# The first transfers and the first scaling step of a two-layer encoder kernel, and the place of ScalarE's squares in its MLP heads

## The chip, the cores and the metric

The kernel runs on one core of a Trainium2 chip. The metric is the device time of one execution in microseconds (us); three timed executions of the kernel before the change gave 1661.46 to 1661.52 us, median 1661.48 us. TensorE (PE) does the matrix products into PSUM, VectorE (DVE) and ScalarE (ACT) evacuate PSUM and prepare operands, GpSimd (POOL) does small side work, SyncE (SP) issues most DMAs; ACT and POOL issue some DMAs too. All times of the trace below are from the span's start.

## What is computed

Two independent sequences of 512 tokens with 1024 features go through two layers with the same weights. Layer 0 mixes by a grouped 2-D Fourier transform, layer 1 by grouped-query attention; each is followed by a squared-ReLU MLP of width 4096, and a final normalisation follows.

```
def sq_relu_mlp(h, w_up, w_down):
    a = jnp.maximum(h @ w_up, 0)
    return (a * a) @ w_down

for i in range(DEPTH):
    if i % N_MIXERS == 0:
        x = x + fourier_mix(rms_norm(x, fourier_norm[j]), fourier_w_out[j])
    else:
        x = x + gqa_attention(rms_norm(x, attn_norm[j]), ...)
    x = x + sq_relu_mlp(rms_norm(x, mlp_norm[i]), mlp_w_up[i], mlp_w_down[i])
return rms_norm(x, final_norm)
```

All data are float32. Most products are made from operands split into a rounded high half and a low rest, as three products of type float32r (high by high, high by low, low by high).

## The kernel before, in words

**The start.** `begin` issues the first loads. SP loads `g` (the gain of the first norm, 128x8 numbers, 4 KB), then the second token tile of `x`, the table `exact[0]` of cosines and sines (128x772), two more token tiles, and the tables `exact[1]` and `exact[2]`; ACT's queue loads the first token tile of `x` (512 KB, into `w`). While these come in, PE runs products of a constant tile with no use for the result (`idle`, line 622; first 12 of them, later 20). Between these two groups PE transposes the broadcast columns of `g` (line 392, 8 products), which puts the gain along the free dimension in PSUM. Then, for the first token tile: ACT squares and sums the row (line 445), POOL raises the mean to the power -0.5 (line 450), DVE multiplies the tile by the gain from PSUM (line 459, two halves), adds the two halves of the features (`plus`, line 463) and subtracts them (`minus`, line 472), and ACT scales the results by the row's factor (`scale_both`, line 484: for the first tile the first 128 columns of the sum, its other 384, 40 picked columns, the difference). The first real products (`exact_even`, line 547) use the scaled sum as weights, 128 columns for each of four output blocks, and the first 258 columns of `exact[0]` as the moving operand. Every instruction of the start is placed by hand, engine by engine.

**The MLP head.** The up product is done by Strassen-like block sums over the two sequences. `first_product` handles 16 pairs of blocks of `w_up`; the first eight form the head. For each pair p of the head, `first` makes the product of the pair's first weight block with `b11` (12 matmuls into one PSUM bank, line 1046) and ACT copies the bank to SBUF (line 1081, `blocks.copied`); `second` then goes on accumulating 12 more matmuls with `b21` into the same bank, so its first matmul must wait until ACT's copy has read the bank. ACT then applies Relu from PSUM (line 1062) and squares the result in place in SBUF (line 1063, `squared`); the square is followed by the DMA that spills it to DRAM for the later down product (line 1059, on ACT's queue). On PE `pair.second` of pair p-1 or p stands between other products, so that PE has matmuls of the next pair to do while ACT copies. For p below 3 the order on PE is that of the code; from there on a scheduler orders every engine's instructions by its own cost model, and `behind(x, y)` only tells it that x is to be placed after y. Before the change, in layer 1 alone and from p = 4 on, pair p-1's square was placed behind pair p's copy.

**The group of two in layer 1's down product.** `second_product` walks over groups of four blocks, one of two in layer 1. `puts` holds the low-half subtractions (line 87, DVE) of operands that were fetched for the next group; for the group of two, the second of the four was placed behind the first row's addition of a PSUM bank into its accumulator (`rows[0].added`, line 1269).

Of the kernel before, what the change touches and what calls it, by code (L numbers as in the profile page):

```python
# [16 lines left out]
ALU = mybir.AluOpType  # L17
# [27 lines left out]
def trunk_kernel(ctx, tc, x_in, xt_in, y_out, tables, rope, gfour, gcol, grow, gfin,  # L45
# [28 lines left out]
    def ps():  # L74
        return psp.tile([P, 512], F32, tag="ps", name=nm("ps"))
# [287 lines left out]

    def exact_table(k):
        t = slot([P, D], F32)
        nc.sync.dma_start(t[:, : tables[k].shape[-1]], tables[k])
        exact.append(t)

    def w_pair(src, n, a):
# [5 lines left out]
    def begin():  # L375
        gr, g = slot([P, D], F32), cons.tile([P, KC], F32, name="g")
        nc.sync.dma_start(g, gfour)
        load_x(0, 0, nc.scalar)
        load_x(0, 1)
        exact_table(4)  # L380
        for t in range(2, 4):
            load_x(0, t)
        exact_table(5)
        exact_table(6)
        nc.scalar.preload_act_table_set("natural_log_exp_and_others")
        idle(ps(), 12)
        halves = []
        for i in range(2):
            o = ps()
            for k in range(4):  # L390
                c = 4 * i + k
                nc.tensor.transpose(o[:, k * P : (k + 1) * P], g[:, c : c + 1].broadcast_to([P, P]), ident)
            halves.append(o)
        return gr, halves
# [36 lines left out]
    class Front:  # L431
# [46 lines left out]
        def scale_both(self, i):  # L478
            if i == 0:
                self.n = exact[0][:, 772:852].rearrange("p (i a b) -> p i a b", i=2, a=5)  # L480
            p, m = self.p[i], self.m[i]
            first = ((p[:, :P], p[:, :P]), (p[:, P:], p[:, P:])) if i == 0 else ((p, p),)
            for out, x in first + ((self.n[:, i], eights(m)), (m, m)):
                nc.scalar.activation(out, x, AF.Copy, scale=self.r[:, i : i + 1])
                yield
            parts.append((self.p[i], self.m[i], self.n[:, i]))
# [310 lines left out]
    with tc.manual_schedule(engines={ET.PE, ET.Activation, ET.DVE, ET.Pool, ET.SP}):  # L797
# [6 lines left out]
        wn.load()  # L804
        idle(ps(), 20)
        for i in range(2):
# [246 lines left out]
    def first_product(l, blocks, rows, ahead, head=iter(())):  # L1053
# [122 lines left out]
        for p in range(AHEAD):  # L1176
# [13 lines left out]
            with tc.manual_schedule(engines={ET.PE}) if p < 3 else nullcontext():  # L1190
                pair.first()
                if l and p > 3:
                    behind(pairs[p - 1].squared, blocks.copied)
# [56 lines left out]
    def second_product(l, blocks, rows, late=lambda: None, ready=lambda m: None, head=iter(())):  # L1250
# [214 lines left out]
        for k, (rows, sums) in enumerate(items):  # L1465
# [46 lines left out]
            if rows and rows[0].n == 2 and len(puts) == 4:  # L1512
                behind(puts[1], rows[0].added)
            for r in rows:
# [730 lines left out]
```

## Time and profile before

| what | value |
|---|---|
| median of three timed executions | 1661.48 us |
| the profiled execution's own time | 1660.31 us |
| its span from first to last instruction | 1658.5 us |
| mean granted TensorE clock | 0.999 |
| busy time PE / weight loads / DVE / ACT / POOL | 1651.5 / 1378.5 / 1265.0 / 878.3 / 394.1 us |
| DMA over the span | 301.43 MB, mean 182 GB/s |

The profiled execution took 1.81 us more than its span and 1.17 us less than the median of the timed ones. A row of the timeline gives the start, the duration, the engine, the line and operation, the tiles it writes and reads without their numbers, its size, the count of instructions merged into it, and in square brackets how long the engine was idle before it and what ended that. "PEld" is the weight load that goes ahead of each matmul; an engine name with a q (SPq) is that engine issuing a DMA. Matmuls are pipelined, so that PE's busy time hides short stalls: a wait shows in the idle time of PEld, and in a stretch that holds fewer matmuls than its length allows.

### The profile page before, as it was taken

The numbers are of one execution on the slowest core, as the hardware profiler recorded it, in microseconds if no ns is written. First come the engines' busy times: TensorE is split into PE (matmuls) and PEld (weight loads), VectorE is DVE, ScalarE is ACT, GpSimd is POOL, SyncE is SP. The second block draws the span as 40 slices with busy tenths as digits, with TensorE's granted clock in tenths as the row PEclk, the third lists the DMA queues.
The fourth block names the chain that finished last, engine by engine and source line by source line (L and its number), as shares of the span: only waits on it lengthen the run. The fifth ranks groups of instructions, "written<-read, shape, count | busy, mean of one in ns | idle before, by whom it ended". The sixth has DMA issues, their size and how long they took to land.

```text
span 1658.5 us, 22101 instructions
## 1 busy us (share of the span) xinstructions
PE 1651.5 (100%) x7762; PEld 1378.5 (83%) x7762; DVE 1265.0 (76%) x1797; ACT 878.3 (53%) x1551; POOL 394.1 (24%) x377
## 2 busy tenths in 40 slices
PE   9999999999999999999999999999999999999998
PEld 8988888888888888888888888888888888888887
DVE  8898785557886779868788888877855487878875
ACT  7776454446243425447688856554554552433335
POOL 5311443222000001325454303004422220000002
PEclk9999999999999999999999999999999999999999
DMA  9843554459775757425501146335544696756632
GB/s 313 241 172 108 196 210 165 146 193 371 229 237 172 246 180 228 177 66 199 166 1 39 65 175 231 127 108 180 201 149 168 226 366 200 233 163 221 186 114 103
DMA packets 121904, 301.43 MB, mean 182 GB/s; under 512 B 12312, under 2 KB 13720, under 8 KB 121792
## 3 DMA queue, kind: packets, MB, share of 16 engines
q1 hardware_dynamic: 98864, 253.66, 43.8%
q0 software_dynamic: 8528, 20.01, 5.7%
q10 hardware_dynamic: 14400, 26.35, 4.2%
q8 instruction: 61, 1.00, 0.2%
q14 instruction: 51, 0.42, 0.1%
HBM read 217.07 MB, written 82.38 MB: 181 GB/s over the span
## 4 chain that ended last, share of the span: by engine, by line
PE 98%; DVE 1%; issue 0%; ACT 0%; DMA 0%; POOL 0%; POOLq 0%; DVEq 0%; ACTq 0%
PE ps L1046 76%; PE ps L83 6%; PE ps L81 6%; PE ps L82 6%; PE ps L1657 2%; PE ps L1636 0%; PE ps L550 0%; PE ps L547 0%; DVE u L2002 0%; DMA g<-gfour 0%; PE ps L217 0%; PE ps L622 0%; PE ps L760 0%; PE ps L1626 0%; PE ps L587 0%
## 5 line engine op out<-in xcount | busy, mean ns | idle before, releaser
L1046 PE MATMUL ps<-u,w 128*128 128x512 f32 x4920 | 1124.6, 389 | 0.0
L1046 PEld LDWEIGHTS ps<-u,w 128*128 128x128 f32 x4920 | 922.7, 188 | 193.8 <-ACT u L1081 1.9
L86 ACT CAST w<-raw 128x1024 fp32r<-128x1024 f32 (+1 forms) x215 | 212.4, 993 | 309.6 <-PE ps L1046 235.9
L87 DVE TENSOR_TENSOR w<-raw,w 128x1024 fp32r<-128x1024 f32 (+1 forms) x215 | 249.3, 1164 | 66.6 <-ACT w L86 62.6
L86 ACT CAST u<-u 128x1024 fp32r<-128x1024 f32 (+1 forms) x140 | 140.7, 1046 | 84.9 <-PE ps L1046 37.4
L87 DVE TENSOR_TENSOR u<-u,u 128x1024 fp32r<-128x1024 f32 (+1 forms) x140 | 168.9, 1233 | 21.6 <-ACT u L86 20.7
L1046 PE MATMUL ps<-u,u 128*128 128x512 f32 x624 | 148.6, 389 | 0.0
L1296 POOL DMA_DIRECT2D raw<-w_sum x32 | 28.1, 879 | 468.5 <-DMA raw<-w_sum 167.6
L1166 POOL TENSOR_TENSOR u<-u 128x512 f32<-128x512 f32 x28 | 37.8, 1351 | 427.6 <-ACT u L1063 427.6
L1269 DVE TENSOR_TENSOR u<-ps,u 128x512 f32<-128x512 f32 x160 | 109.4, 685 | 36.8 <-PE ps L1046 34.0
L1046 PEld LDWEIGHTS ps<-u,u 128*128 128x128 f32 x624 | 117.1, 188 | 24.3
L81 PE MATMUL ps<-u,u 128*128 128x512 f32 (+2 forms) x342 | 129.0, 379 | 0.0
L83 PE MATMUL ps<-u,u 128*128 128x512 f32 (+2 forms) x342 | 124.5, 364 | 0.0
L82 PE MATMUL ps<-u,u 128*128 128x512 f32 (+2 forms) x342 | 124.2, 363 | 0.0
L177 POOL TENSOR_TENSOR t<-t,t 128x512 f32<-128x512 f32 (+1 forms) x47 | 67.5, 1441 | 187.2 <-ACT t L171 163.2
L1062 ACT ACTIVATE t<-t 128x512 f32<-128x512 f32 x64 | 40.5, 632 | 111.4 <-DVE t L1135 101.4
L87 DVE TENSOR_TENSOR u<-ps,u 128x512 fp32r<-128x512 f32 (+3 forms) x112 | 68.1, 635 | 7.3 <-ACT u L86 6.9
L83 PEld LDWEIGHTS ps<-u,u 128*128 128x128 f32 x342 | 64.3, 188 | 10.5 <-DVE u L87 0.4
L82 PEld LDWEIGHTS ps<-u,u 128*128 128x128 f32 x342 | 64.6, 189 | 8.5 <-DVE u L87 0.7
L81 PEld LDWEIGHTS ps<-u,u 128*128 128x128 f32 x342 | 64.7, 189 | 7.8
L1122 DVE TENSOR_TENSOR t<-ps,u 128x512 f32<-128x512 f32 x32 | 22.0, 687 | 60.9 <-PE ps L1046 50.3
L86 ACT CAST u<-ps 128x512 fp32r<-128x512 f32 (+3 forms) x112 | 59.4, 558 | 9.6 <-PE ps L1657 7.6
(270 smaller groups left out, 2013.3 us busy)
## 6 DMA issues: line engine op xcount, KB each, us to landing
raw<-w_up SPq DMA_DIRECT2D x80, 512.0 KB, 4.6
u<-spill_t SPq DMA_DIRECT2D x60, 512.0 KB, 7.0
raw<-w_sum SPq DMA_DIRECT2D x56, 512.0 KB, 5.6
u<-spill_b SPq DMA_DIRECT2D x45, 512.0 KB, 6.4
spill_t<-u SPq DMA_DIRECT2D x84, 256.0 KB, 2.0
spill_b<-t ACTq DMA_DIRECT2D x60, 256.0 KB, 4.2
raw<-w_row SPq DMA_DIRECT2D x28, 512.0 KB, 4.8
park<-u SPq DMA_DIRECT2D x24, 512.0 KB, 3.9
```

What stands on the lines that cost most here:

```text
L81: nc.tensor.matmul(out, lh, rh, start=first, stop=False)
L82: nc.tensor.matmul(out, lh, rl, start=False, stop=False)
L83: nc.tensor.matmul(out, ll, rh, start=False, stop=last)
L86: hi = nc.scalar.copy(dst_hi, src)
L87: return hi, eng.tensor_sub(dst_lo, src, f32(dst_hi))
L177: nc.gpsimd.tensor_add(acc[q][:, :n], acc[q][:, :n], s[:, :n])
L1046: nc.tensor.matmul(o, w[x][:, sl], h[k][y], start=first and k + i == 0, stop=k == n - 1 and i == 2, skip_group_check=not first)
L1062: nc.scalar.activation(t, src, AF.Relu)
L1166: eng.tensor_sub(t[:, 0], b12, b11)
L1269: return nc.vector.tensor_add(x, o, x)
L1296: nc.gpsimd.dma_start(s[:, 1], w[:, 3], accum_op=ALU.add)
L1657: nc.tensor.transpose(pt[:, t * P : (t + 1) * P], probs[t][:, sc * P : (sc + 1) * P], ident)
```

## The change

Three places are edited.

1. **The start.** `g` is loaded by ACT's queue and the first token tile by SP's, first of all. `exact_table` can load a table in pieces; the first 258 columns of `exact[0]` are now loaded ahead of the second token tile and the other 514 behind it. The idle products are 10 and 21 instead of 12 and 20. Of the first tile's four scaling steps, the first (128 columns of the sum) goes to DVE, where it stands behind `minus` of the same tile; the other steps stay on ACT.
2. **The MLP heads.** In both layers, from p = 3 on, pair p-1's square stands behind pair p's copy.
3. **The group of two.** All four of `puts`, not only the second, stand behind `rows[0].added`.

```diff
-    def exact_table(k):
+    def exact_table(k, cuts=()):
         t = slot([P, D], F32)
-        nc.sync.dma_start(t[:, : tables[k].shape[-1]], tables[k])
         exact.append(t)
+        edges = [0, *cuts, tables[k].shape[-1]]
+        for c0, c1 in zip(edges, edges[1:]):
+            nc.sync.dma_start(t[:, c0:c1], tables[k][:, c0:c1])
+            yield
...
     def begin():
-        nc.sync.dma_start(g, gfour)
-        load_x(0, 0, nc.scalar)
+        nc.scalar.dma_start(g, gfour)
+        load_x(0, 0)
+        pieces = exact_table(4, (258,))
+        next(pieces)
         load_x(0, 1)
-        exact_table(4)
+        for _ in pieces:
+            pass
...
-        idle(ps(), 12)
+        idle(ps(), 10)
...
-            for out, x in first + ((self.n[:, i], eights(m)), (m, m)):
-                nc.scalar.activation(out, x, AF.Copy, scale=self.r[:, i : i + 1])
+            for j, (out, x) in enumerate(first + ((self.n[:, i], eights(m)), (m, m))):
+                if i == j == 0:
+                    nc.vector.tensor_scalar(out, x, self.r[:, :1], None, ALU.mult)
+                else:
+                    nc.scalar.activation(out, x, AF.Copy, scale=self.r[:, i : i + 1])
                 yield
...
-        idle(ps(), 20)
+        idle(ps(), 21)
...
                 pair.first()
-                if l and p > 3:
+                if p > 2:
                     behind(pairs[p - 1].squared, blocks.copied)
...
             if rows and rows[0].n == 2 and len(puts) == 4:
-                behind(puts[1], rows[0].added)
+                for y in puts:
+                    behind(y, rows[0].added)
```

On SP's queue at the start of the program these are the first rows before (`u_109` is the second token tile, `u_111` the table `exact[0]`, `u_113` and `u_115` the third and fourth tile, `u_117` the table `exact[1]`):

```order
L377 DMA g<-gfour 128x8
L352 DMA u_109<-x 128x1024
L366 DMA u_111<-xtab 128x772
L352 DMA u_113<-x 128x1024
L352 DMA u_115<-x 128x1024
L366 DMA u_117<-xtab 128x770
```

And these now (`w_106` is the first token tile, `u_109` now the table, `u_111` the second token tile):

```order
L352 DMA w_106<-x 128x1024
L369 DMA u_109<-xtab 128x258
L352 DMA u_111<-x 128x1024
L369 DMA u_109<-xtab 128x514
L352 DMA u_114<-x 128x1024
L352 DMA u_116<-x 128x1024
```

The first token tile has come from ACT's queue to the head of SP's, a third of the table stands ahead of the second token tile, and `g` has gone to ACT's queue.

On ACT in layer 0's head, around pairs 3 and 4 (`u_1417`, `u_1457` and `u_1491` are the results of pairs 2, 3 and 4, `ps_` their banks; L1062 and L1063 are Relu and square, L1081 the copy), before:

```order
L1062 ACTIVATE u_1417<-ps_1418 128x512
L1059 DMA spill_b_0_1274<-u_1357 128x512
L1063 ACTIVATE u_1417<-u_1417 128x512
L1081 COPY u_1457<-ps_1458 128x512
L1059 DMA spill_b_0_1274<-u_1417 128x512
L86 CAST w_1584<-raw_1582 128x1024
L1062 ACTIVATE u_1457<-ps_1458 128x512
L86 CAST w_1630<-raw_1578 128x1024
L1063 ACTIVATE u_1457<-u_1457 128x512
L1081 COPY u_1491<-ps_1492 128x512
```

And now (L1072, L1073 and L1091 are the same three lines):

```order
L1072 ACTIVATE u_1417<-ps_1418 128x512
L1069 DMA spill_b_0_1274<-u_1357 128x512
L1091 COPY u_1457<-ps_1458 128x512
L1073 ACTIVATE u_1417<-u_1417 128x512
L1069 DMA spill_b_0_1274<-u_1417 128x512
L86 CAST w_1584<-raw_1582 128x1024
L1072 ACTIVATE u_1457<-ps_1458 128x512
L86 CAST w_1630<-raw_1578 128x1024
L1091 COPY u_1491<-ps_1492 128x512
L1073 ACTIVATE u_1457<-u_1457 128x512
```

Each square has changed places with the copy behind it.

On PE in the same head, between the last matmuls of pair 4's first product (weights from `u_1072` and `w_1488`, bank `ps_1492`) and the first of its second (`u_1092`), there stood six matmuls of pair 5 (`ps_1536`):

```order
L1046 MATMUL ps_1492<-u_1073,w_1488 128x512
L1046 MATMUL ps_1492<-u_1072,w_1488 128x512
L1046 MATMUL ps_1536<-u_1052,w_1532 128x512
L1046 MATMUL ps_1536<-u_1053,w_1532 128x512
L1046 MATMUL ps_1536<-u_1052,w_1532 128x512 x2
L1046 MATMUL ps_1536<-u_1053,w_1532 128x512
L1046 MATMUL ps_1536<-u_1052,w_1532 128x512
L1046 MATMUL ps_1492<-u_1092,w_1488 128x512
```

Now there stand four:

```order
L1056 MATMUL ps_1492<-u_1073,w_1488 128x512
L1056 MATMUL ps_1492<-u_1072,w_1488 128x512
L1056 MATMUL ps_1536<-u_1052,w_1532 128x512
L1056 MATMUL ps_1536<-u_1053,w_1532 128x512
L1056 MATMUL ps_1536<-u_1052,w_1532 128x512 x2
L1056 MATMUL ps_1492<-u_1092,w_1488 128x512
```

The scheduler has moved the second product two matmuls closer to the copy it waits for. The same count falls from six to four for pair 3 and from 14 to seven for pair 5 of layer 0; in layer 1 it falls from five to four for pair 3, stays at four for pair 4 and falls from six to five for pair 5.

More of the change, by code (lines that the diff above doesn't have):

```diff
@@ L376, in begin @@
         gr, g = slot([P, D], F32), cons.tile([P, KC], F32, name="g")
-        nc.sync.dma_start(g, gfour)
-        load_x(0, 0, nc.scalar)
+        nc.scalar.dma_start(g, gfour)
+        load_x(0, 0)
+        pieces = exact_table(4, (258,))
+        next(pieces)
         load_x(0, 1)
-        exact_table(4)
+        for _ in pieces:
+            pass
         for t in range(2, 4):
             load_x(0, t)
-        exact_table(5)
-        exact_table(6)
+        for k in (5, 6):
+            for _ in exact_table(k):
+                pass
         nc.scalar.preload_act_table_set("natural_log_exp_and_others")
-        idle(ps(), 12)
+        idle(ps(), 10)
         halves = []
```

## The prediction

> **What bounds the kernel now.** I read the page first, then who waits for whom among PE's weight loads, then the chain that ended last for the two heads, and last the timeline of the three places that the change touches. The page:
>
> ```profile
> span 1658.5 us, 22101 instructions
> ...
> PE 1651.5 (100%) x7762; PEld 1378.5 (83%) x7762; DVE 1265.0 (76%) x1797; ACT 878.3 (53%) x1551; POOL 394.1 (24%) x377
> ...
> PE 98%; DVE 1%; issue 0%; ACT 0%; DMA 0%; POOL 0%; POOLq 0%; DVEq 0%; ACTq 0%
> ```
>
> PE is busy all through, and the chain that ended last is 98% PE. The change leaves the number of useful matmuls as it is, so it can only move the moment at which PE's useful work starts, and the stalls inside PE's stream. The waits of the weight loads, in all the span, show how little there is of these:
>
> ```profile
> PEld ps L1046 <- ACT u L1081: 1.9, 7, 0.4
> PEld ps L622 <- DVE w L347: 1.2, 1, 1.2
> PEld ps L82 <- DVE u L87: 0.7, 4, 0.2
> ...
> PEld ps L547 <- ACT t L484: 0.2, 1, 0.2
> ```
>
> The first row is the wait that the squares' new place is about: seven times, 1.9 us in all, a second product of an MLP head waits for ACT's copy of the bank. Of the start there are 1.2 us ahead of the first idle product and 0.2 us ahead of the second block of the first real product (line 547); the 0.7 us for line 87 lie outside the touched places. No wait of the down products of layer 1 (DVE, line 87 or 1269) is in the list. So the whole field for a gain is about 2 us, or 0.1%. A measurement of this kernel can tell about 0.2% (3.3 us) from no change; the forecast is no change.
>
> **The start.** The timeline:
>
> ```profile
> 0.72 0.41 ACTq L352 DMA_DIRECT2D w<-x  x1
> 0.73 0.39 SPq L377 DMA_DIRECT2D g<-gfour  x1
> ...
> 1.16 2.93 PE L622 MATMUL ps<-u 128*128 128x256 f32 x12 [1.16 <-DVE w L347]
> ...
> 4.32 1.23 PE L392 MATMUL ps<-ident,g 128*128 128x128 f32 x8 [0.23 <-DMA g<-gfour]
> 4.89 1.06 ACT L445 ACTIVATE w<-w 128x1025 bf16<-128x1025 f32 x1 [2.44 <-DMA w<-x]
> 5.16 1.28 DVE L459 TENSOR_TENSOR u<-w,ps 128x512 f32<-128x512 f32 x2 [3.99 <-PE ps L392]
> ...
> 5.31 2.64 PE L622 MATMUL ps<-u 128*128 128x256 f32 x20
> ...
> 6.12 1.06 ACT L445 ACTIVATE t<-u 128x1024 bf16<-128x1024 f32 x1
> 6.20 0.57 POOL L450 TENSOR_TENSOR s<-s,half 128x1 f32<-128x1 f32 x1 [3.72 <-ACT w L445]
> ...
> 7.08 0.68 DVE L472 TENSOR_TENSOR t<-u 128x512 f32<-128x512 f32 x1
> ...
> 7.26 0.91 ACT L484 ACTIVATE t<-t,s 128x128 f32<-128x128 f32 x2
> ...
> 7.68 1.28 DVE L459 TENSOR_TENSOR u<-u,ps 128x512 f32<-128x512 f32 x2
> ...
> 7.79 2.00 PE L547 MATMUL ps<-u,t 128*128 128x257 f32 x8
> ...
> 8.22 1.16 PEld L547 LDWEIGHTS ps<-u,t 128*128 128x128 f32 x6 [0.21 <-ACT t L484]
> ```
>
> PE's transposes wait for `g`, DVE for the transposes, and DVE then works without a pause to the end of `minus` at 7.08 + 0.68 = 7.76. ACT squares when the first token tile has landed, and scales at 7.26 because its second square (6.12 + 1.06, and reading the sum) is in front. The first real matmul runs at 7.79, behind the last idle product and the first scaling.
>
> Scaling on DVE: it is free for that at 7.68 (where its next row starts now), POOL's power is long done (6.77). No 128-column step of this kind is in the trace; the same operation on wider tiles is:
>
> ```profile
> L2092 DVE TENSOR_SCALAR u<-u,s 128x512 f32<-128x512 f32 x1 | 0.5, 481 | 0.0
> ...
> L2092 DVE TENSOR_SCALAR u<-u,s 128x256 f32<-128x256 f32 x1 | 0.4, 353 | 0.3 <-POOL s L1984 0.3
> ```
>
> 128 columns more or less cost half of 481 - 353 = 128 ns, so 128 columns take about 353 - 64 = 289 ns: done at 7.97, and the first real matmul at about 8.02 instead of 7.79, 0.23 us later. Against that, ACT, rid of one of the two steps that take 0.91 us from 7.26 on, has the other 384 columns done before PE asks for the second block, and the wait of 0.21 us at 8.22 is gone; as the weight loads run ahead, the stream gains less than the wait, about 0.1 us. So with the transfers as they are the start loses 0.1 to 0.2 us; I take +0.15. ACT's second square comes later, since 258 of the table's columns (128 x 258 x 4 bytes, 132 KB) now precede the second token tile: 0.3 us at the 416 GB/s that the stretch from 4.3 to 7.8 moved (the last number of the first row below). That costs ACT what the dropped scaling saves it, and PE is not reached: the second square would end at 7.5 and the 384 columns be done by about 8.2, when PE's second block, now at 8.22, would ask for them at 8.4.
>
> ```profile
> 4.30:7.80 3.50, 3.48 (x29) 3.50 (x29) 2.61 (x5) 2.83 (x6) 1.02 (x2) 1.00 1.02 416
> ...
> w<-x ACTq DMA_DIRECT2D x1, 512.0 KB, 4.1
> ...
> g<-gfour SPq DMA_DIRECT2D x1, 4.0 KB, 3.5
> ```
>
> The exchange of the two queues is the unknown. `g` took 3.5 us to land from SP, the tile 4.1 us from ACT. If it is the queue that makes the difference, `g` lands 0.6 us later, and with it transposes, DVE and the first real matmul: +0.6 on top of +0.15. The other end is that `g` and the tile both land 0.6 us sooner: -0.6, about what ten idle products instead of twelve (2 x 0.244 = 0.49) leave room for. I take no change: both were issued in the same hundredth of a microsecond, and what differs is that the tile has 128 times the bytes. [...] The second row of DVE's chain and every later one come 0.2 us later too; they feed PE's next products, and what cover they lose is counted in the bound of +0.75 for the whole start.
>
> **The heads.** In layer 0 pair 4's second product, and in layer 1 pair 3's, wait for a copy that stands behind a square (the rows at 112.58 and 1052.69 are the squares):
>
> ```profile
> 112.58 0.63 ACT L1063 ACTIVATE u<-u 128x512 f32<-128x512 f32 x1
> ...
> 113.11 0.57 ACT L1081 COPY u<-ps 128x512 f32<-128x512 f32 x1
> ...
> 113.73 0.77 PEld L1046 LDWEIGHTS ps<-u,w 128*128 128x128 f32 x4 [0.33 <-ACT u L1081]
> ...
> 1052.69 0.63 ACT L1063 ACTIVATE u<-u 128x512 f32<-128x512 f32 x1
> ...
> 1053.85 0.53 PEld L1046 LDWEIGHTS ps<-u,w 128*128 128x128 f32 x3 [0.33 <-ACT u L1081]
> ...
> 1058.53 0.59 ACT L1081 COPY u<-ps 128x512 f32<-128x512 f32 x1
> ...
> 1059.17 0.53 PEld L1046 LDWEIGHTS ps<-u,w 128*128 128x128 f32 x3 [0.20 <-ACT u L1081]
> ```
>
> What such a wait costs the stream is less than its length, as the weight loads run ahead. I read it from short stretches of PE alone around each of the three, with the mean length of a matmul from the page and a long undisturbed piece of the chain:
>
> ```profile
> 113.43 1.28 PE L1046 MATMUL ps<-u,w 128*128 128x512 f32 x4
> ...
> 1053.32 1.27 PE L1046 MATMUL ps<-u,w 128*128 128x512 f32 x4
> ...
> 1058.78 1.35 PE L1046 MATMUL ps<-u,w 128*128 128x512 f32 x5
> ...
> 1044.61 560.93 PE ps L1046 x2472
> ...
> L1046 PE MATMUL ps<-u,w 128*128 128x512 f32 x4920 | 1124.6, 389 | 0.0
> ```
>
> From start to start a matmul takes 560.93 / 2472 = 0.2269 us. Four of them, less the last one's 0.389, should take 3 x 0.2269 = 0.68 us; they took 1.28 - 0.389 = 0.89 at pair 4 of layer 0 and 0.88 at pair 3 of layer 1. So the touched waits cost 0.21 and 0.20 us, 0.41 together. PE's new order gives a part back. The last pair of rows, of layer 1's pair 4, is a case with four matmuls between the products and no square ahead of the copy: the copy starts as soon as the product has ended, and PE still waits 0.20 us on it, which by the row at 1058.78 costs 1.35 - 0.389 - 4 x 0.2269 = 0.05. With four between them, pairs 3 and 4 of layer 0 and pair 3 of layer 1 come to this state: 0.15 us lost. The squares' own delay costs nobody: behind a square stand only its spill, and casts whose results PE needs microseconds later. Sum of the heads -0.41 + 0.15 = -0.26 us, with bounds of -0.46 (no wait is left at the touched places, and pair 4 of layer 1 loses its 0.05) and +0.2 (the three new cases cost 0.2 each, as a wait behind a square did).
>
> **The group of two.** DVE's four subtractions slip behind the first row's addition:
>
> ```profile
> 1505.28 1.22 DVE L87 TENSOR_TENSOR u<-u,u 128x1024 fp32r<-128x1024 f32 x1
> ...
> 1508.74 0.68 DVE L1269 TENSOR_TENSOR t<-ps,t 128x512 f32<-128x512 f32 x1
> ```
>
> The first of the four ran at 1505.28; in the new order it stands right behind the addition of 1508.74, and the last seven rows later. On PE 36 matmuls (8.2 us at 0.2269) stand between the product that the addition reads and the first use of the first operand, and 24 more ahead of the second: cost 0. Without that cover it would be one subtraction, 1.2 us; nothing on PE waits for DVE here now, so a gain is excluded.
>
> **The sum.** +0.15 for the start, -0.26 for the heads, 0.0 for the group of two: -0.1 us. Against the profiled execution (1660.31 us) that gives 1660.2; the timed median stands 1.17 us above that execution, so the forecast is 1661.48 - 0.1 = 1661.4 us. The bounds give -0.6 - 0.46 = -1.06 and +0.75 + 0.2 = +0.95, from 1660.4 to 1662.4.
>
> **The rivals.** *Both loads land sooner and the heads' waits vanish.* For it speaks that PE idles 0.23 us for `g` and DVE 3.99 us for the transposes; against it, the bytes of the two loads and the four-matmul case above. It gives -0.6 - 0.41 = -1.0, 1660.5 us.
>
> *`g` lands late from ACT's queue.* For it speaks the 4.1 us of that queue's only early load, against it the bytes of that load. It gives +0.75 - 0.26 = +0.5, 1662.0 us.
>
> *PE's clock comes up later.* The idle products run slow at first and fast later: 2.93 / 12 = 0.244 us each in the first group, 2.64 / 20 = 0.132 in the second. Now the first group ends two products, 0.49 us, sooner, so the idle time ahead of the transposes grows from 0.23 to about 0.7 us if `g` lands as before. If that gap keeps PE slow through the second group, its 21 products cost 21 x (0.244 - 0.132) = 2.35 us more, and all that follows is that much later: 1661.4 + 2.35 = 1663.7 us, slower than before, though still within 0.2%. It decides when the gap is long enough to count as a pause; the trace has no gap of this length in a slow stretch. [...]
>
> *The squares' move brings nothing*, because the scheduler spends all of it on the shorter distance: the upper bound of the heads, +0.2, with the start 1661.8 us. Layer 1's pair 4 speaks against it, where the shorter distance costs 0.05.
>
> **How the numbers follow.** No change beyond some tenths, the forecast and the squares' rival together: 0.66. Both gains: 0.16. Late `g`: 0.11. Late clock: 0.05. Left over, 0.02: a load order that starves PE in the first 30 us. The range 1660.4 to 1662.4 holds the first three. Faster by more than 3.3 us has no mechanism in the list of waits: 0.01. Slower by more than that needs the late clock together with late loads: 0.03. Within 0.2%: 0.96.
>
> **What would show it.** Right: the transposes at 4.3, the first real matmul near 8.0 without the 0.21 us wait behind it; DVE's new step under 0.3 us at 7.7; waits of about 0.2 us on the copy at pairs 3 and 4 of layer 0 and pair 3 of layer 1, and those of 0.33 us gone; no wait for line 87 near 1515 us. Wrong: transposes at 3.9 or 4.9 (the queues), idle products of the second group at 0.24 us (the clock), or any new wait on PE over 0.5 us.

## The result, and the profile after

The changed kernel takes 1663.53 us (median of 22 runs, 1662.78 to 1664.93), the kernel before 1661.28 us beside it (22 runs, 1660.42 to 1662.64): ratio 1.0015, 95% interval 1.0009 to 1.0021. It is slower by 2.25 us, and the interval leaves 1 out. That is less than the 0.2% that the prediction took for the least difference that can be told; 22 runs against 22 tell about 0.06%. The forecast was 1661.4 us with a range up to 1662.4; the loss lies outside.

The profiled execution took 1664.78 us, 4.47 more than that of before, so it shows more than the medians do, and what differs from execution to execution has to be kept apart from what the change does. The page of the changed kernel (its line numbers are 7 to 10 higher than before: idle products at 632 instead of 622, transposes at 399, the MLP's products at 1056, the copy at 1091, the addition at 1279):

```profile
span 1663.0 us, 22095 instructions
...
PE 1654.2 (99%) x7761; PEld 1380.4 (83%) x7761; DVE 1266.2 (76%) x1798; ACT 878.3 (53%) x1550; POOL 395.0 (24%) x377
...
PE 94%; DVE 3%; DMA 1%; issue 1%; ACT 0%; POOL 0%; POOLq 0%; DVEq 0%; ACTq 0%; SPq 0%
```

The chain that ended last was 98% PE and is now 94%, with 3% on DVE. The waits of the weight loads over the whole span (us in total, times, the longest):

```profile
PEld ps L1056 <- ACT u L1091: 1.8, 8, 0.4
PEld ps L1056 <- DVE w L87: 1.7, 2, 1.0
PEld ps L399 <- issue: 1.3, 1, 1.3
PEld ps L632 <- DVE w L347: 1.2, 1, 1.2
PEld ps L560 <- issue: 0.8, 2, 0.4
PEld ps L1056 <- DVE t L1279: 0.8, 2, 0.6
```

The wait for the copies is nearly as long as before (1.9 us, seven times). New are the second and the sixth row, in which PE waits for DVE in the down products. The third row, ahead of the transposes, has grown; in the kernel before it was

```profile
PEld ps L392 <- issue: 0.5, 1, 0.5
```

**The start.** The timeline of the changed kernel:

```profile
1.16 2.50 PE L632 MATMUL ps<-u 128*128 128x256 f32 x10 [1.16 <-DVE w L347]
...
4.45 1.06 ACT L452 ACTIVATE w<-w 128x1025 bf16<-128x1025 f32 x1 [2.00 <-DMA w<-x]
...
4.71 1.94 PE L399 MATMUL ps<-ident,g 128*128 128x128 f32 x8 [1.05 <-DMA g<-gfour]
...
6.30 4.59 PE L632 MATMUL ps<-u 128*128 128x256 f32 x21
...
6.84 1.06 ACT L452 ACTIVATE t<-u 128x1024 bf16<-128x1024 f32 x1 [1.24 <-DMA u<-x]
...
8.62 0.28 DVE L492 TENSOR_SCALAR t<-t,s 128x128 f32<-128x128 f32 x1
...
10.73 1.46 PE L557 MATMUL ps<-u,t 128*128 128x257 f32 x6
```

ACT starts on the first tile 0.44 us sooner (4.45 against 4.89), PE on the gain 0.39 later (4.71 against 4.32). PE pauses 1.05 us ahead of the transposes instead of 0.23, and then runs more slowly than before: the transposes take 1.94 us instead of 1.23, and the second group's idle products 4.59 / 21 = 0.219 us each instead of 0.132. DVE's scaling takes 0.28 us and is done at 8.90, but the first real matmul waits behind the slow idle products until 10.73, 2.94 us later than before. The second token tile came later as well (6.84 against 6.12).

**The heads**, pairs 3 and 4 of layer 0 and pair 3 of layer 1:

```profile
109.91 0.59 ACT L1091 COPY u<-ps 128x512 f32<-128x512 f32 x1 [0.85 <-PE ps L1056]
...
110.40 0.63 ACT L1073 ACTIVATE u<-u 128x512 f32<-128x512 f32 x1
...
110.55 5.31 PEld L1056 LDWEIGHTS ps<-u,w 128*128 128x128 f32 x24 [0.20 <-ACT u L1091]
...
116.06 1.91 PEld L1056 LDWEIGHTS ps<-u,w 128*128 128x128 f32 x9 [0.20 <-ACT u L1091]
...
1056.67 5.31 PEld L1056 LDWEIGHTS ps<-u,w 128*128 128x128 f32 x24 [0.19 <-ACT u L1091]
```

Each copy now runs ahead of the square, and the waits are 0.19 and 0.20 us where two of them were 0.33. From the starts of the matmuls in the trace, each of these costs PE's stream 0.05 us, against 0.19 at both places before.

**The group of two.** Here is DVE from the additions near 1530 us on, and the matmuls that wait for it:

```profile
1534.39 0.69 DVE L1279 TENSOR_TENSOR t<-ps,t 128x512 f32<-128x512 f32 x1 [2.03 <-PE ps L1056]
...
1535.00 1.22 DVE L87 TENSOR_TENSOR u<-u,u 128x1024 fp32r<-128x1024 f32 x1
...
1536.73 1.22 DVE L87 TENSOR_TENSOR u<-u,u 128x1024 fp32r<-128x1024 f32 x1
...
1543.71 6.05 PE L1056 MATMUL ps<-u,w 128*128 128x512 f32 x26
...
1549.11 1.22 DVE L87 TENSOR_TENSOR w<-raw,w 128x1024 fp32r<-128x1024 f32 x1
...
1550.38 1.89 PE L1056 MATMUL ps<-u,w 128*128 128x512 f32 x7 [0.62 <-DVE w L87]
```

And the same place in the kernel before:

```profile
1528.67 2.35 DVE L87 TENSOR_TENSOR u<-u,u 128x1024 fp32r<-128x1024 f32 x2
1530.94 0.68 DVE L1269 TENSOR_TENSOR t<-ps,t 128x512 f32<-128x512 f32 x1
...
1540.10 12.18 PE L1046 MATMUL ps<-u,w 128*128 128x512 f32 x53
...
1543.99 1.22 DVE L87 TENSOR_TENSOR w<-raw,w 128x1024 fp32r<-128x1024 f32 x1
```

Before, DVE made two subtractions (the 2.35 us) while PE still worked on the bank that the next addition reads. Now the addition stands ahead of these two, and DVE waits 2.03 us for PE with both behind it. The low half w_13864 (the last DVE row of each fence) is wanted 26 matmuls after the start of the row at 1543.71, at 1543.71 + 26 x 0.2269 = 1549.61; it is done at 1549.11 + 1.22 = 1550.33, 0.72 us late, and PE loses 0.89 us by the starts of its matmuls. In the kernel before it was done at 1545.21 and wanted at 1540.10 + 26 x 0.2269 = 1546.00. Near 1513 us there is another stall of 0.46 us, where a second product waits for an addition that stands behind a subtraction that waits for ACT's cast.

The sum for these two executions: start +2.84 (measured at the first stall of the MLP head, 104.59 against 101.75 us), heads -0.24, group of two +0.89 and +0.46, and +0.48 at 676 us in layer 0's down product, where the order is the same in both kernels: 4.43 us of the 4.5 by which the spans differ.

### The profile page after: what moved, and what is told of

It reads as the page before. It is cut to its first block, busy times and chain, and to the rows that moved or that the text cites. A ratio compares the mean times of both kernels' runs of the same rounds, so it can differ in the third digit from the quotient of the medians.

```text
span 1663.0 us, 22095 instructions
## 1 busy us (share of the span) xinstructions
PE 1654.2 (99%) x7761; PEld 1380.4 (83%) x7761; DVE 1266.2 (76%) x1798; ACT 878.3 (53%) x1550; POOL 395.0 (24%) x377
## 4 chain that ended last, share of the span: by engine, by line
PE 94%; DVE 3%; DMA 1%; issue 1%; ACT 0%; POOL 0%; POOLq 0%; DVEq 0%; ACTq 0%; SPq 0%
PE ps L1056 72%; PE ps L83 6%; PE ps L81 6%; PE ps L82 6%; PE ps L1668 2%; DMA u<-w_qkv 1%; DVE u L87 1%; DVE w L87 0%; PE ps L1647 0%; PE ps L560 0%; DVE u L1279 0%; PE ps L557 0%; DVE u L2013 0%; PE ps L632 0%; DMA g<-gfour 0%
## 5 line engine op out<-in xcount | busy, mean ns | idle before, releaser
L1072 ACT ACTIVATE t<-t 128x512 f32<-128x512 f32 x64 | 40.4, 632 | 111.3 <-DVE t L1145 101.2
```

The costliest lines, as they stand in the source:

```text
L1072: nc.scalar.activation(t, src, AF.Relu)
```

## The experiments

Each kernel was timed 11 times, in turns with 33 runs of the kernel before on the same chip. Differences are of medians; the interval of a ratio is about +-0.0009 (1.5 us) wide, so what is smaller is read from the profiles.

| run | median, us | before beside it | difference | ratio, 95% |
|---|---|---|---|---|
| e1 start only | 1662.45 | 1661.2 | +1.25 | 1.0001 to 1.0019 |
| e2 heads only | 1660.35 | 1661.2 | -0.85 | 0.9988 to 1.0006 |
| e3 group of two only | 1662.18 | 1661.2 | +0.98 | 0.9997 to 1.0015 |
| e4 start and heads | 1662.42 | 1661.2 | +1.22 | 1.0002 to 1.0019 |
| e5 queues alone | 1661.11 | 1661.02 | +0.09 | 0.9991 to 1.0009 |
| e6 start, old queues | 1661.55 | 1661.02 | +0.53 | 0.9994 to 1.0012 |
| e7 low half early | 1661.94 | 1661.02 | +0.92 | 0.9998 to 1.0015 |
| e8 three of four | 1661.37 | 1661.02 | +0.35 | 0.9993 to 1.001 |
| e9 subtractions first | 1662.81 | 1661.16 | +1.65 | 1.0 to 1.0018 |
| e10 addition first | 1661.69 | 1661.16 | +0.53 | 0.9993 to 1.0011 |
| e11 table cut alone | 1661.07 | 1661.16 | -0.09 | 0.9992 to 1.001 |
| e12 heads, short idle | 1660.8 | 1661.16 | -0.36 | 0.9988 to 1.0005 |
| e13 later rows restored | 1661.53 | 1660.98 | +0.55 | 0.9995 to 1.0013 |
| e14 start, no pause | 1661.93 | 1660.98 | +0.95 | 0.9997 to 1.0015 |
| e15 pause made | 1662.01 | 1660.98 | +1.03 | 0.9998 to 1.0015 |
| e16 heads, 14 and 16 idle | 1660.73 | 1660.98 | -0.25 | 0.9992 to 1.0009 |

### The three edits apart

Theory A put the loss into the start, theory B into the group of two. e1 is the change with the second and third edit taken back; e2 and e3 are the kernel before with one edit each; e4 is the change with the third taken back.

```diff
 e1 and e4, on the changed kernel
-                for y in puts:
-                    behind(y, rows[0].added)
+                behind(puts[1], rows[0].added)
 e1 besides
-                if p > 2:
+                if l and p > 3:
 e2, on the kernel before
-                if l and p > 3:
+                if p > 2:
 e3, on the kernel before
-                behind(puts[1], rows[0].added)
+                for y in puts:
+                    behind(y, rows[0].added)
```

e1:

> Only the first edit (loads, table in pieces, 10 and 21 idle products, DVE's scaling). Theory A (the lost time is in the start: the late gain leaves a gap ahead of the transposes and PE's clock comes up late, first real matmul at 10.7 us instead of 7.8): +2 to +2.9 us against the kernel before. Theory B (the lost time is in the group of two of layer 1's down product, 1.4 us in the changed kernel's trace; the late clock is an accident of the profiled execution): +0.3 to +0.8 us, the late gain alone. The prediction's own term was +0.15.

e2:

> Only the second edit (the squares behind the copies from p = 3 on, in both layers). Both theories: -0.24 us, the waits of 0.33 us at pair 4 of layer 0 and pair 3 of layer 1 shortened to 0.2 us, each of which costs 0.05. The prediction's term was -0.26.

e3:

> Only the third edit (all four low-half subtractions behind the first row's addition in the group of two). Theory A: 0 to +0.3 us. Theory B: +1.4 us, with 0.5 us of it where the second product on the bank waits for the addition (near 1513 us) and 0.9 us where a low half comes late from DVE (near 1550 us). The prediction's term was 0.

e4:

> The changed kernel without the third edit. Theory A: +1.8 to +2.6 us against the kernel before, the same as the changed kernel. Theory B: +0.1 to +0.6 us, the changed kernel less 1.4 us.

Measured +1.25, -0.85, +0.98 and +1.22. Both theories are half right, and e1, e3 and e4 lie between their forecasts: e4 and e3 together give 2.20 of the 2.25 us. By the intervals e1 and e4 are clear of no change, e3 by itself is not. The heads bring what was forecast by their rows (in e2 all five waits cost 0.05 to 0.1 us, and the two of 0.19 are gone); the timing can't tell that from nothing (e2 -0.85 us, but e4 only 0.03 under e1). In e3, whose start is that of before, the stall near 1548 us is there in full:

```profile
1541.01 6.05 PE L1046 MATMUL ps<-u,w 128*128 128x512 f32 x26
...
1547.68 2.56 PE L1046 MATMUL ps<-u,w 128*128 128x512 f32 x10 [0.62 <-DVE w L87]
```

Its matmul was wanted at 1541.01 + 26 x 0.2269 = 1546.91 and ran at 1547.68. The other stall of the changed kernel, 0.46 us near 1513, is missing here, and profiles without the whole third edit have stalls between 1495 and 1528 too (five of 13: e10 1.06 us, e14 0.63, e11 0.36, e15 0.33, e16 0.17). In the changed kernel DVE waits there at a subtraction that the third edit put ahead of the addition; e3 has the same wait of DVE, 1.29 us, and no stall of PE behind it. So that stall isn't laid to the change, and whether the new order adds to it stays open.

### The start: queues, table, pause

e5 is the kernel before with the queues of `g` and the first tile exchanged; e6 is e1 with the exchange undone; e11 has only the table in two pieces.

```diff
 e5, on the kernel before
-        nc.sync.dma_start(g, gfour)
-        load_x(0, 0, nc.scalar)
+        nc.scalar.dma_start(g, gfour)
+        load_x(0, 0)
 e6, on e1
-        nc.scalar.dma_start(g, gfour)
-        load_x(0, 0)
+        nc.sync.dma_start(g, gfour)
+        load_x(0, 0, nc.scalar)
 e11, on the kernel before (besides exact_table, as in the change)
...
-        load_x(0, 1)
-        exact_table(4)
+        pieces = exact_table(4, (258,))
+        next(pieces)
+        load_x(0, 1)
+        for _ in pieces:
+            pass
```

e5:

> The kernel before with nothing but the exchange of the queues: the gain on ACT's queue, the first token tile on SP's. Theory Q (the exchange makes the gain late, and the gap on PE keeps its clock down): transposes at 4.6 to 4.9 us instead of 3.9 to 4.3, the second group of idle products slow for at least a part of it, +0.5 to +1.0 us against the kernel before. Rival R (the exchange is harmless; the shorter first idle group, the cut table and DVE's scaling cost the time): transposes by 4.3 us, 0 to +0.3 us.

e6:

> The first edit with the queues of the kernel before (gain first on SP, first token tile on ACT); table in pieces, 10 and 21 idle products and DVE's scaling stay. Theory Q: transposes at 3.9 to 4.3 us, first real matmul at 8.0 to 8.6 us, +0.1 to +0.5 us against the kernel before. Rival R: the same loss as the whole first edit, +1.2 us.

e11:

> Of the first edit only the cut table: its first 258 columns ahead of the second token tile. The prediction had the tile 0.3 us later and hidden. Theory T (the tile lands 0.7 to 1.7 us later, as in the profiles of the whole first edit): ACT's second square at 6.8 to 7.8 us instead of 6.1, and with it ACT's first scaling and the first real matmul at 8.4 to 9.4, +0.6 to +1.6 us. Rival: the tile 0.3 us later, 0 to +0.2 us.

In e5 the gain is as late as in the changed kernel, the pause 0.55 us, and yet PE's clock came up in time (full from 4.70 us, see the table below):

```profile
4.63 1.09 PE L392 MATMUL ps<-ident,g 128*128 128x128 f32 x8 [0.55 <-DMA g<-gfour]
...
5.48 2.63 PE L622 MATMUL ps<-u 128*128 128x256 f32 x20
...
7.95 2.01 PE L547 MATMUL ps<-u,t 128*128 128x257 f32 x8
```

Theory Q is right that the gain comes later from ACT's queue (transposes from 4.62 to 4.85 us in the five profiles with it there, at 4.57 or sooner in the thirteen with it on SP, in five of these at 3.74 to 3.89 with no wait). From issue to landing it took 3.8 to 4.0 us there, 2.8 to 3.7 from SP. Its price and the late clock did not come: the exchange alone cost 0.09 us, as rival R has it. In e6 there was no pause, and the loss had another place:

```profile
7.78 1.06 ACT L452 ACTIVATE t<-u 128x1024 bf16<-128x1024 f32 x1 [2.27 <-DMA u<-x]
...
8.06 0.62 PE L557 MATMUL ps<-u,t 128*128 128x257 f32 x2
...
8.83 0.60 ACT L494 ACTIVATE t<-t,s 128x384 f32<-128x384 f32 x1
...
9.48 1.35 PE L557 MATMUL ps<-u,t 128*128 128x257 f32 x5 [0.80 <-ACT t L494]
```

ACT had the second token tile at 7.78 us; in the kernel before it was there by 6.12. On ACT the square of that tile (1.06 us from 7.78 on) is ahead of the scaling of the first tile's other 384 columns, which starts at 8.83, and PE's second block waits 0.80 us for those. The prediction had the tile 0.3 us later and covered. e11 was to show that the cut does it, and didn't: the tile came at 6.24 with a wait of 0.41 us, and the time is that of before. In the six profiles with the cut table the DMA engines moved 275 to 390 GB/s from 3.5 to 6.5 us, in the twelve without it 391 to 418. Less was moved in the profiles with the late tile, then, but e11, with the same loads as e6, has 390; whether the cut is the cause, and what makes it vary, stays open.

e14 closes the pause in the changed start, e15 makes one in the old start.

```diff
 e14, on e1
-        idle(ps(), 10)
+        idle(ps(), 14)
 e15, on the kernel before
-        idle(ps(), 12)
+        idle(ps(), 8)
```

e14:

> The first edit with 14 instead of 10 idle products in the first group, which end at 4.58 us, when the gain lands on ACT's queue. Theory C (the pause of about 1 us ahead of the transposes keeps PE's clock down through the second group): pause under 0.35 us, first real matmul at 8.0 to 9.1 us instead of 9.5 to 10.7, +0.2 to +0.7 us against the kernel before. Rival D (the late gain, the later second token tile and DVE's scaling cost the time without the clock): +1.0 to +1.4 us, as the whole first edit.

e15:

> The kernel before with 8 instead of 12 idle products in the first group, which end at 3.1 us; the gain stays first on SP's queue and lands at 3.7 to 4.4. Theory C: a pause of 0.6 to 1.3 us, slow idle products in the second group, first real matmul at 8.8 to 10.5 us, +0.5 to +1.5 us against the kernel before. Rival D: transposes as early as the gain allows, 0 to +0.2 us.

e15, whose loads are those of before and whose only edit is four idle products fewer:

```profile
1.16 2.08 PE L622 MATMUL ps<-u 128*128 128x256 f32 x8 [1.16 <-DVE w L347]
...
3.88 1.94 PE L392 MATMUL ps<-ident,g 128*128 128x128 f32 x8 [0.65 <-DMA g<-gfour]
...
5.48 4.27 PE L622 MATMUL ps<-u 128*128 128x256 f32 x20
...
9.58 1.68 PE L547 MATMUL ps<-u,t 128*128 128x257 f32 x7
```

The transposes start 0.44 us sooner than in the profile of before, and the first real matmul still comes 1.79 later, behind idle products of 4.27 / 20 = 0.214 us. Timed it costs 1.03 us, with an interval that reaches just below 1. With the old loads, a pause of 0.65 us in PE's warm-up went with a late clock (full from 9.18 us), as theory C has it. e14 answers from the other side, and only by half. The pause is 0.29 us, the idle products are fast (2.75 / 21 = 0.131 us each), the first real matmul is at 8.36 instead of 9.5 to 10.7:

```profile
4.81 1.08 PE L399 MATMUL ps<-ident,g 128*128 128x128 f32 x8 [0.29 <-DMA g<-gfour]
...
5.64 2.75 PE L632 MATMUL ps<-u 128*128 128x256 f32 x21
...
7.50 1.06 ACT L452 ACTIVATE t<-u 128x1024 bf16<-128x1024 f32 x1 [1.78 <-DMA u<-x]
...
8.36 0.70 PE L557 MATMUL ps<-u,t 128*128 128x257 f32 x2
...
9.21 1.57 PE L557 MATMUL ps<-u,t 128*128 128x257 f32 x6 [0.15 <-ACT t L494]
```

But +0.95 us are left, between the two forecasts. With the clock in time, the late gain and the late second tile come to the path, as in e6 (the last row waits for ACT's 384 columns). Not all of the 0.95 is the start: this profile has 0.63 us of stalls near 1511 and 1522 besides. The two costs stand in each other's shadow: timed apart, the pause gave 1.03 us (e15) and what is left without it 0.53 (e6) and 0.95 (e14), more than 1.25 together; none of the three is clear of no change by its interval. DVE's scaling and the one idle product more in the second group were not run alone.

The moment of the full clock is in the record of the granted clock that the trace holds; in the views it shows only by the pace of the idle products (in the kernel before 2.93 / 12 = 0.244 us each in the first group, 2.64 / 20 = 0.132 in the second, with the full clock from 4.69 us on). It varies from execution to execution with an unchanged start as well:

| profiles | pause ahead of the transposes, us | full clock from, us | first real matmul, us |
|---|---|---|---|
| old start: before, e2, e3, e7, e8, e9, e10, e13 | 0 to 0.30 | 4.69, 4.83, 6.71, 6.82, 4.49, 7.36, 5.89, 6.03 | 7.79, 7.62, 8.56, 8.52, 7.45, 9.05, 8.41, 8.19 |
| e6, e11, e12, e16 | under 0.1, 0, 0.48, 0 | 5.65, 5.36, 7.33, 6.56 | 8.06, 8.00, 8.51, 8.23 |
| e5, e14 | 0.55, 0.29 | 4.70, 4.85 | 7.95, 8.36 |
| e15 | 0.65 | 9.18 | 9.58 |
| e1, e4, after | 1.19, 0.96, 1.05 | 7.60, 9.38, 10.47 | 9.54, 10.21, 10.73 |

The old start, and every profile with a pause of 0.55 us or less, has the full clock between 4.49 and 7.36 us; those with a pause of 0.65 or more have it between 7.60 and 10.47. The first real matmul comes at 8.20 us on average in the old start and at 10.16 in the last row. The timed difference of e1 is 1.25, not 1.96; three profiles are few, and I take the timing for the size and the profiles for the mechanism. That a pause delays the clock rests on these 18 profiles.

The length of the pause does not set the moment by itself: with 0 to 0.30 us it lies anywhere between 4.49 and 7.36 us, and e1, with the longest pause, 1.19 us, has the earliest full clock of the last row, 7.60 us. What sets it within these ranges was not shown.

### The group of two: what on DVE makes the low half late

Theory G: the low half w_13700, which slips three rows, frees its raw slot late, and what is loaded into it reaches PE late. Rival H: anything else.

```diff
 e7, on e3: the last two subtractions behind that low half too (low: the low halves of a row's weights)
...
+                        while held_back and nrows:
+                            behind(held_back.pop(), nrows[0].low[0])
...
+                held_back += puts[2:]
 e8, on the kernel before
-                behind(puts[1], rows[0].added)
+                for y in puts[1:]:
+                    behind(y, rows[0].added)
```

e7:

> The third edit alone, but the last two of the four subtractions are put behind the low half w_13700 as well, so that DVE makes that low half three rows sooner than with the third edit. Theory G (that low half's slip frees its raw slot late, and the loads and sums behind it reach PE late near 1550 us): the stall of 0.9 us near 1548 to 1550 us is gone, 0 to +0.2 us against the kernel before. Rival H (the four subtractions or the cast's wait ahead of the addition cost the time by themselves): the stall stays or another of 0.5 us or more takes its place, +0.6 to +1.2 us.

e8:

> The third edit for the last three of the four subtractions only. DVE's rows from the group's end on stand as in the kernel before, but the low half w_13700 stands three rows later, and the subtraction of u_13621 ahead of the addition. Theory G: a stall of 0.4 to 0.9 us near 1548 us, +0.4 to +1.0 us. Rival H, the reordered rows behind the group as the cause: no stall there, 0 to +0.2 us.

Theory G falls twice: in e7 the low half is early and the stall stays (0.72 us), in e8 it is late and there is none in the profile (timed +0.35, between the two forecasts). What e8 keeps of the kernel before, and e7 doesn't, is the order of DVE's rows 40 us on, near 1530. That gave theory J: the addition that waits for PE in front of two subtractions. e9, e13 and e10 turn that order:

```diff
 e9, on e3
+            if l and k == 11:
+                for y in puts[:2]:
+                    behind(rows[0].added, y)
 e13, on e3: the same for both additions there (the lines that record sums.added left out)
...
+            if l and k == 11:
+                for x in (rows[0].added, sums.added[0]):
+                    for y in puts[:2]:
+                        behind(x, y)
 e10, on the kernel before: the order turned the other way
+            if l and k == 11:
+                for y in puts[:2]:
+                    behind(y, rows[0].added)
```

e9:

> The whole third edit, and one order more: in the step that follows two steps later, the two low-half subtractions u_13765 and u_13768 stand ahead of the addition that waits for the bank ps_13740, as in the kernel before. Theory J (the loss comes from that addition: it waits 2.0 us for PE with the two subtractions behind it, and what DVE could have done then is missing near 1548 us): no wait of 2.0 us on DVE near 1530 us, no stall of 0.9 us near 1548 us, 0 to +0.2 us against the kernel before. Rival K (the later place of the four subtractions and of w_13700 is enough): the stall stays at 0.5 us or more, +0.6 to +1.1 us.

e10:

> The third edit left out, but the addition that waits for the bank ps_13740 put ahead of the two subtractions u_13765 and u_13768, as the third edit made it. Theory J: DVE waits about 2 us at that addition and PE 0.4 to 0.9 us near 1547 us, +0.4 to +1.0 us. Rival K: no stall, 0 to +0.2 us.

e13:

> The whole third edit, with the two subtractions u_13765 and u_13768 ahead of both additions that wait for PE near 1530 us, which is DVE's order of the kernel before at that place; the four subtractions and w_13700 stay late. Theory J (DVE's work behind a waiting addition is what reaches PE late near 1548 us): no stall there, 0 to +0.4 us against the kernel before. Rival K (the late place of the four subtractions and of w_13700 is enough by itself): a stall of 0.5 us or more near 1548 us, +0.6 to +1.1 us.

e9 failed as a test: the scheduler set another addition between the two subtractions, and DVE waited there.

```profile
1529.65 1.21 DVE L87 TENSOR_TENSOR u<-u,u 128x1024 fp32r<-128x1024 f32 x1
1533.13 0.69 DVE L1269 TENSOR_TENSOR u<-ps,u 128x512 f32<-128x512 f32 x1 [2.26 <-PE ps L1046]
1533.73 1.22 DVE L87 TENSOR_TENSOR u<-u,u 128x1024 fp32r<-128x1024 f32 x1
1534.87 0.69 DVE L1269 TENSOR_TENSOR t<-ps,t 128x512 f32<-128x512 f32 x1
...
1535.61 3.02 PE L1046 MATMUL ps<-u,w 128*128 128x512 f32 x12 [1.16 <-DVE t L1269]
```

The addition at 1534.87, which could have run behind the first subtraction (its product ends six matmuls, 1.4 us, ahead of the one that DVE waits for), holds a bank on which PE's second product then waits: a stall of 1.43 us at 1535.6, and +1.65 us timed. It shows the same thing from another side: what stands on DVE behind a row that waits for PE, 2.26 us here, comes late with it. e10 has the wait of 2.03 us of e3 and no stall near 1547 us, against theory J's word; its +0.53 us lie within that theory's range by accident, as its profile has 1.06 us of stalls before 1524:

```profile
1532.39 0.69 DVE L1269 TENSOR_TENSOR t<-ps,t 128x512 f32<-128x512 f32 x1 [2.03 <-PE ps L1046]
...
1545.37 1.82 DVE L87 TENSOR_TENSOR w<-raw,w 128x512 fp32r<-128x512 f32 x2
```

Here the scheduler put w_13864 one subtraction further ahead (the row of 1.82 us holds it and the one before it), which gave 1.1 us back. And e13 has no wait of 2.0 us but 0.52 us of the stall (timed +0.55, between the two forecasts):

```profile
1538.04 0.69 DVE L1269 TENSOR_TENSOR t<-ps,t 128x512 f32<-128x512 f32 x1 [0.67 <-PE ps L1046]
...
1546.86 5.51 PE L1046 MATMUL ps<-u,w 128*128 128x512 f32 x23 [0.25 <-DVE w L87]
```

So neither theory holds alone. (e8's profile is the fastest of its eleven runs, 1660.12 us, while three of them take 1663.2 to 1663.4; it shows that the order can do without the stall, not where those three lose. e7's is the slowest of its eleven.) What the seven profiles agree on is the end of w_13864 on DVE against the time at which PE wants it, worked out as above (26 matmuls behind the row of the products that lead to it):

| kernel | w_13864 done, us | wanted, us | late by | stall, us |
|---|---|---|---|---|
| before | 1545.21 | 1546.00 | -0.79 | 0 |
| e8 | 1545.18 | 1545.83 | -0.65 | 0 |
| e10 | 1547.19 | 1547.61 | -0.42 | 0 |
| e13 | 1546.81 | 1546.46 | 0.35 | 0.52 |
| e7 | 1549.58 | 1549.03 | 0.55 | 0.72 |
| e3 | 1547.62 | 1546.91 | 0.71 | 0.89 |
| after | 1550.33 | 1549.61 | 0.72 | 0.89 |

The kernel before had 0.8 us to spare. All four subtractions put back use it up and 0.7 more, through several new orders of DVE's rows in the 40 us behind. The stall is in four of the five profiles with the whole third edit and in none of the 13 without it; the fifth, e9, has its own of 1.43 us, and its w_13864 is done 1.56 us ahead of need. Which of the new rows between 1513 and 1545 us cost how much of the slack stays open.

### The heads alone, with other idle groups

Since the heads alone show no loss, two kernels add to them a shorter second idle group, which should cost less where the clock comes late.

```diff
 e12, on e2
-        idle(ps(), 20)
+        idle(ps(), 14)
 e16, on e2
-        idle(ps(), 12)
+        idle(ps(), 14)
...
-        idle(ps(), 20)
+        idle(ps(), 16)
```

e12:

> The second edit, and 14 instead of 20 idle products in the second group. Where PE's clock comes up late, the second group of 20 ends at 8.5 us, about 0.6 us behind the first scaling (three profiles with the old start); 14 end 0.8 to 1.3 us sooner. Theory: the first real matmul follows the scaling, at 7.5 to 8.0 us in every execution; -0.24 us for the heads and 0 to -0.5 for the group, together -0.3 to -0.7 against the kernel before. Rival: the pause that the shorter group leaves ahead of the first real matmul keeps the clock down for longer, and the first real products run slow: +0.3 to +1.0 us.

e16:

> The second edit with 14 idle products in the first group and 16 in the second. Theory C: no pause ahead of the transposes, so the clock comes up no later than before, and the shorter second group costs less where it comes late; -0.24 us for the heads and 0 to -0.4 for the start, -0.2 to -0.6 us in all. Rival: the longer first group delays transposes and gain by up to 0.5 us where the gain lands early: 0 to +0.3 us.

-0.36 and -0.25 us, and e2 -0.85: all three medians lie under that of the kernel before beside them, where the changed kernel's lies 2.25 us above, but none can be told from before by its interval. e12's profile missed its theory: the first real matmul came at 8.51 us instead of 7.5 to 8.0, behind a gain that let the transposes start only at 4.57. e12's eleven runs lie within 0.7 us (1660.56 to 1661.26), where the sets of 22 and 33 runs of the kernel before spread over 2.2 to 3.4 and the 11 of e2 over 3.0: the long times are missing, and so are the short ones (e2's shortest is 1659.64). With eleven runs this can be chance.

## Why the prediction was wrong, step by step

- **The bound** held: PE is still it. But the list of waits of before bounds a gain (2 us, and more with the rows of lines 392, 550 and 554 that it did not name); how much cover a row has before it becomes a wait, no row of it says, and both losses came from used-up cover.
- **DVE's scaling, +0.15** held in its row: 0.28 us against 0.289 worked out from wider tiles.
- **"I take no change" for the exchange of the queues** failed as a landing and held as a price: the gain came at 4.62 to 4.85 us instead of 3.7 to 4.6, the first tile hardly sooner (ACT's first square at 4.37 to 4.61 from SP, 4.32 to 5.14 from ACT), and the exchange alone cost 0.09. The reason given, the bytes, is answered by the landings: on ACT's queue the 4 KB landed 0.2 to 0.3 us after the 512 KB issued within 0.01 us on SP's, in all five profiles, and on SP's queue 0.6 to 0.8 us ahead of the tile on ACT's in all thirteen.
- **The second token tile 0.3 us later, not reaching PE** failed: ACT's square of it started 0.7 to 1.8 us later than in the kernel before in five of six profiles, and where the clock was in time (e6, e14) PE waited 0.80 and 0.15 us for the 384 columns behind ACT's square of that tile.
- **The late clock, chance 0.05, 1663.7 us** was the rival that happened in the start, though at a pause of 1 us where it had named 0.7. Its mechanism fits e15 and the profiles (with a pause of 0.65 us or more the full clock comes at 7.60 to 10.47 us, with less at 4.49 to 7.36), its chance, which no row of before gave, was far too low: the cut from 12 to 10 idle products and the late gain were each costed by themselves, and their sum, a pause of 1 us, was taken for a rare case. It is in all three profiles with the changed start. Of its price, 2.35 us, about half appears in the timing (e1, +1.25), since the old start loses some of it too in many executions (its first real matmul came at 7.45 to 9.05 us in eight profiles). That its 1663.7 us stands near the measured 1663.53 is luck: about 1 us of the loss came from the group of two.
- **The heads, -0.26** held by the rows: -0.24 by the starts of the matmuls, each new case at the 0.05 us taken from layer 1's pair 4. By these rows the rival that the squares' move brings nothing falls; the timing is too coarse for it.
- **The group of two, "cost 0"** failed: +0.98 us alone as timed, 0.89 by the stall in e3's profile. The step counted the matmuls up to the first use of the four operands, and these were never late. It did not follow the scheduler's rows behind them, where DVE's order changed for 40 us and ate the 0.8 us of slack, and 0.7 us more, of a low half that the edit doesn't name.
- **The sum**: as timed apart it was start +1.2, heads -0.2 by their rows, group +1.0. The range left out a case that the text had as a rival and had no case at all for the group.

## What to carry to other kernels

When a constraint is given to a scheduler, the cost is not in the instructions it names: compare the whole row order of each engine until it is the same again, and ask of every row that waits for another engine what now stands behind it (here DVE waited 2.03 us at an addition with two subtractions behind it, and PE lost 0.89 us at a low half that the edit doesn't name). Cutting warm-up work and delaying what follows it are one change, a longer pause (1.05 us here instead of 0.23, with the full clock at 10.47 us instead of 4.69), and are priced together. A cost that differs from execution to execution should be read from several profiles of kernels that share that stage before one profile is called the state of things.

## What the runs showed of the hardware that was not expected

- A pause of 0.65 us, 2.1 us after PE's first product began, went with a full clock at 9.18 us, where the eight profiles of the old start have 4.49 to 7.36; one of 0.55 us (e5) went with 4.70.
- The gain, 4 KB, took 3.8 to 4.0 us from issue to landing on ACT's queue (five profiles) and 2.8 to 3.7 on SP's (thirteen), with a 512 KB load issued beside it on the other queue each time. Why is open.
- In layer 0's down product, with the same order, PE stalled near 671 to 677 us by 0 (most profiles) to 1.9 us (e7), waiting for low halves from DVE. With the start (up to 1.6 us between profiles of the old start) and the stalls near 1495 to 1528 us (up to 1.06), this is of the size of the spread of over 2 us between the times of one kernel; that it makes up all of it is not shown.
